# Nine dummy products, first loads on two queues, and a last token tile summed in two halves of its columns, in a two-layer hybrid encoder

## The chip, the cores and the metric

The kernel runs on 1 core of one Trainium2 chip. The metric is the time on the device in microseconds (us) from one launch to its end. Each kernel was run several times; the number that stands for it is the median. One further execution was recorded by the hardware profiler, and every row of a view below comes from that one.

## The reference

A trunk of two layers works on one stream x of 256 tokens by 2048 features, all in 32-bit floats.

```python
def even_layer(x, ...):                       # layer 0
    hn = rmsnorm(x, norm_g)
    q, k, v, u, z_a, z_b = jnp.split(hn @ w_in, cuts, axis=-1)   # 1024 columns each
    o_a = chunked_relpos_attention(q, k, v, rel_bias) * jax.nn.silu(z_a)
    y = jax.nn.gelu(s5_ssm(u, lam_re, lam_im, log_dt, b_re, b_im, c_re, c_im, d_skip))
    o_b = y * jax.nn.sigmoid(y @ w_glu + b_glu) * jax.nn.silu(z_b)
    return x + jnp.concatenate([o_a, o_b], axis=-1) @ w_out

def odd_layer(x, ...):                        # layer 1
    hn = rmsnorm(x, norm_g)
    q, k, v, z, f_logit = jnp.split(hn @ w_in, cuts, axis=-1)    # 2048 columns each, 16 for f
    log_f = jax.nn.log_sigmoid(f_logit + b_forget)
    o = forgetting_attention(q, k, v, log_f) * jax.nn.silu(z)
    return x + o @ w_out

out = rmsnorm(odd_layer(even_layer(x)), final_norm_g)
```

`s5_ssm` is a state space model: 64 groups of 16 channels of u, each with 64 complex states that a recurrence over the 256 tokens carries on. The large matrices (w_in of both layers, w_out of both, w_glu) are what the kernel streams from memory; the attention, the recurrence and the norms are small beside them.

## The kernel before

**Tiling.** The tokens lie in two tiles of 128 (t = 0 and 1). A weight matrix is read in column blocks of 512 (`NT`); along the 2048 rows it comes in chunks of two blocks of 128 rows (`CK`), so one chunk is a tile of 128 x 1024 numbers, 512 KB. `next_w` loads the next chunk on SyncE's (SP's) queue into `wr` (4 buffers), and splits it into a rounded part `wh` (ScalarE, ACT, L164) and the rest `wl` (VectorE, DVE, L165), 3 buffers each. Where an activation has been split in the same way (`xTh`, `xTl`), the product in full precision is the sum of three products on TensorE (PE): high by high (L175), high by low (L176), low by high (L177). `project` makes these for 16 blocks of rows and both token tiles and adds them up in two accumulators of 128 x 512; every name `acc_...` is one of these. A chunk feeds 12 products.

**Front.** The first chunk comes in two halves of 256 KB (`split`), each with its own splits, so that the first products can start sooner. `gE` is the norm's weight; `x_block` scales the transposed x (`xTr`) by it and splits it (L215, L216). The norm's factor for each token is applied later, to the sums. All these loads stand on SP. The S5 part reads its parameters (`lr`, `li`, `dt`, `dcol`) through GpSimd's (POOL's) queue in `s5_setup`.

**Order.** PE runs its instructions in the order in which the program is written. On the other engines a scheduler lays them out when the kernel is built, by modelled times, and gives the splits a high priority. Work beside the stream of weights is cut into tasks; `tick` advances one step after each chunk, and `at_chunk` places a task on that clock. Such a task's products stand on PE between two chunks.

**The order of the work up to 100 us.** First come the two column blocks of u (`acc_u`). Their sums are scaled into `ut` tiles (one to a token tile and column block) and stored to a buffer `u_d` in memory (L743 and L747). Four loads on SP read it back in another layout as `un` (L439), ACT reorders it (L446, `spread`), and PE transposes it (`pu`, L456). Beside this run the tables of the S5 part (`tables`): DVE computes `mx` (L378 to L380), which SP stores (`m_d`, L381); PE multiplies it with `bb` into `pk` (L395); DVE and ACT make `ks` of that, which SP stores as `k_d` (L402); loads of `bc` (L340) for a later table stand behind these stores on SP, and ACT scales them (L356). Meanwhile PE goes on with the projections for za (`acc_za`) and then q.

**The tail.** The last projection is w_out of layer 1, its last column block with `by_token=True`: its eight chunks are held ready, and the 48 products of tile 0 are made before the 48 of tile 1. Then `add_tile` adds the sum to x (L997) and squares it on ACT (L999), and the final norm's factor follows in five small steps (`ms`, `r` by a power on POOL, `c`, `rc`, L1022 to L1027). The last 512 columns (`xg`) and the three other column blocks are multiplied by `rc` and stored, four stores of 256 KB on SP to a token tile (L1034).

Of the kernel before, what the change touches and what calls it, by code (L numbers as in the profile page):

```python
# [9 lines left out]
F32 = mybir.dt.float32  # L10
F32R = mybir.dt.float32r
AF = mybir.ActivationFunctionType
# [5 lines left out]
P = 128  # L18
L = 256
# [18 lines left out]
PI_F = 3.1415925  # L38
SPLIT_AHEAD = 3000
SCAN_SLOW, S5_OUT = 79, 95  # L40


@with_exitstack
def trunk(ctx: ExitStack, tc: tile.TileContext, a, out: bass.AP):
# [8 lines left out]

    ctx.enter_context(tc.manual_schedule(engines={mybir.EngineType.PE}))

    warm = const.tile([P, 1], F32, name="warm")
    nc.vector.memset(warm, 0.0)
    nc.scalar.activation(warm, warm, AF.Exp)
    gE = const.tile([P, 16], F32, name="gE")
    nc.sync.dma_start(gE, a["gE"])  # L60
    xin = a["x"].rearrange("(t p) d -> p t d", p=P)

    ident = const.tile([P, P], F32, name="ident")
# [84 lines left out]
    def next_w(split=None, dst=None):  # L148
# [8 lines left out]
        step = NT if split else CK * NT  # L157
        for o in range(0, CK * NT, step):
            c = slice(o, o + step)
            nc.sync.dma_start(raw[:, c], a["w"][i][:, c])  # L160
            if split:
                split(o // NT)
            with tc.high_priority(offset=SPLIT_AHEAD):
                last_split[:] = [nc.scalar.activation(wh[:, c], raw[:, c], AF.Copy)]  # L164
                nc.vector.tensor_tensor(wl[:, c], raw[:, c], wh[:, c].bitcast(F32), op=ALU.subtract)  # L165
        return wh, wl

    def project(ah, al, nkb, name, evac, ready=None, by_token=False):
# [8 lines left out]
            nc.tensor.matmul(acc[t], sl, wh[:, c], start=False, stop=kb == nkb - 1)  # L177

        if by_token:
            for t in range(2):  # L180
                for kb in range(nkb):
                    block(kb, *ready[kb // CK], t)
            return acc
        for kc in range(nkb // CK):
            wh, wl = ready[kc] if ready else next_w()
            kbs = range(kc * CK, (kc + 1) * CK)
# [70 lines left out]
    cr = sm("cr")  # L257
    csn = s5.tile([P, 2, G], F32, name="csn")
    kst = [s5.tile([P, 2, 2 * P], F32, name=f"ks{i}") for i in range(2)]
    e2 = s5b.tile([P, 2, G], F32, name="e2")  # L260
    e1t = s5b.tile([P, G], F32, name="e1t")

    def s5_setup():
        for h in range(2):
            nc.gpsimd.dma_start(lr[h * 64:(h + 1) * 64, :], a["s5lr"])
            nc.gpsimd.dma_start(li[h * 64:(h + 1) * 64, :], a["s5li"])
        nc.gpsimd.dma_start(dt, a["s5dt"].to_broadcast([P, G]))
        dcol = s5.tile([P, NGQ], F32, name="dcol")
        nc.gpsimd.dma_start(dcol, a["s5d"])
        for t_ in kst:  # L270
            nc.gpsimd.memset(t_[:, :, 0:P], 0.0)

        V.memset(sgn[0:64, :], -1.0)
        V.memset(sgn[64:128, :], 1.0)
        V.memset(nsgn[0:64, :], 1.0)
# [740 lines left out]
    held = [next_w(dst=(lh[:, i, :], ll[:, i, :]) if i < 4 else None if i < 7 else lx) for i in range(8)]  # L1016
    acc = project(oTh, oTl, 16, "oo3", None, held, by_token=True)
    for t in range(2):
        xs = add_tile(3, acc[t], t)
        xg = l1.tile([P, NT], F32, name=f"xg_{t}", tag="xg")  # L1020
        nc.vector.tensor_tensor(xg, xs, gF[:, 3 * NT:], op=ALU.mult)
        ms, r, c, rc = (const.tile([P, 1], F32, name=f"{w}_2{t}") for w in ("ms", "rs", "rc", "rr"))  # L1022
        nc.vector.scalar_tensor_tensor(ms, ssp2[:, t, 3:4], 1.0 / D, s012[:, t:t + 1], op0=ALU.mult, op1=ALU.add)
        nc.gpsimd.tensor_tensor(r, ms, mhalf[:, 0:1], op=ALU.pow)
        nc.vector.tensor_scalar(c, ms, r, r, op0=ALU.mult, op1=ALU.mult)
        nc.vector.tensor_scalar(c, c, -0.5, 1.5, op0=ALU.mult, op1=ALU.add)
        nc.vector.tensor_tensor(rc, r, c, op=ALU.mult)  # L1027
        for n in (2, 3, 0, 1):
            xs = x[:, t, n * NT:(n + 1) * NT] if n < 3 else xg
            if n == 2:  # L1030
                nc.scalar.activation(xs, xs, AF.Copy, scale=rc)
            else:
                nc.vector.tensor_scalar(xs, xs, rc, None, op0=ALU.mult)
            nc.sync.dma_start(ov[:, t, n * NT:(n + 1) * NT], xs)  # L1034

# [75 lines left out]
```

## Time and profile before

| | before |
|---|---|
| runs, us | 968.22, 966.23, 968.06 |
| median, us | 968.06 |
| the profiled execution's own time, us | 967.27 |
| its span (first to last instruction), us | 965.6 |
| mean granted clock of PE, as a share of full speed | 0.99 |
| moved by the DMA engines | 190.43 MB, 197 GB/s on average |

The profile's second part cuts the span into 40 slices of 24.1 us and gives the busy share of an engine in tenths (9 is 90% or more):

```
PE   6997999999998999999999999999999999999995
ACT  6636556864464666455645644464446444644451
PEclk9999999999999899999999999999999999999998
DMA  9877566645999468655556555555554556455552
```

PE's lower digits stand in the first slice, in the fourth (72 to 97 us), in the thirteenth (290 to 314 us) and in the last. In the views, a row of the timeline has the start and the length of an instruction in us, its engine, line, operation, and what it writes and reads; a bracket gives the idle time before it and what ended that. A length of a product on PE runs from its issue to its end, and products overlap: what one costs is the distance to the next one's start, not its length.

### The profile page before, as it was taken

To read this page: it belongs to the slowest core of one execution; us is meant where nothing else is said; L and a number is where in the kernel's file an instruction comes from. 1 tells how busy PE (TensorE), PEld (TensorE's weight loads), DVE (VectorE), ACT (ScalarE), POOL (GpSimd) and SP (SyncE) were. 2 spreads that over 40 slices of the span, in tenths; PEclk is the share of its full clock that TensorE was granted. 3 is DMA by queue.
4 is the path that set the end of the run, shared out by engine and by line. 5 is a ranking of instruction groups with operands and counts; after the bars stand their busy time and mean duration, and the time that the engine had idled before them with its cause. 6 is when DMAs were issued, how large, how long until landed. Compare 5 with 4: busy or idle time off the path is not lost.

```text
span 965.6 us, 13241 instructions
## 1 busy us (share of the span) xinstructions
PE 933.5 (97%) x4814; PEld 758.8 (79%) x4814; DVE 579.4 (60%) x1023; ACT 517.0 (54%) x817; POOL 104.4 (11%) x177
## 2 busy tenths in 40 slices
PE   6997999999998999999999999999999999999995
PEld 5885777777776678788888888888888888888884
DVE  7886678755798346665755545454545454545573
ACT  6636556864464666455645644464446444644451
POOL 2000000000652000200001400040004000200210
PEclk9999999999999899999999999999999999999998
DMA  9877566645999468655556555555554556455552
GB/s 326 289 222 230 178 203 203 193 156 185 227 232 305 161 224 247 219 174 182 179 195 226 174 186 174 190 171 186 173 193 148 184 173 194 152 182 171 195 197 88
DMA packets 68546, 190.43 MB, mean 197 GB/s; under 512 B 7936, under 2 KB 22512, under 8 KB 68096
## 3 DMA queue, kind: packets, MB, share of 16 engines
q1 hardware_dynamic: 65056, 181.07, 58.4%
q0 software_dynamic: 3424, 8.51, 3.5%
q8 instruction: 38, 0.62, 0.3%
q14 instruction: 28, 0.23, 0.1%
HBM read 180.09 MB, written 9.45 MB: 196 GB/s over the span
## 4 chain that ended last, share of the span: by engine, by line
PE 85%; DVE 4%; DMA 3%; ACT 3%; issue 3%; SPq 1%; POOL 0%; POOLq 0%; DVEq 0%; ACTq 0%
PE acc_cq L175 3%; PE acc_cv L177 3%; PE acc_ck L175 3%; PE acc_cq L177 3%; PE acc_cv L176 3%; PE acc_cz L177 3%; PE acc_cv L175 3%; PE acc_cq L176 3%; PE acc_cz L175 3%; PE acc_ck L177 3%; PE acc_ck L176 3%; PE acc_cz L176 3%; PE acc_oo L177 3%; PE acc_oo L175 3%; PE acc_oo L176 3%
## 5 line engine op out<-in xcount | busy, mean ns | idle before, releaser
L165 DVE TENSOR_TENSOR wl<-wr,wh 128x1024 fp32r<-128x1024 f32 (+1 forms) x292 | 361.4, 1238 | 288.1 <-ACT wh L164 287.4
L164 ACT ACTIVATE wh<-wr 128x1024 fp32r<-128x1024 f32 (+1 forms) x292 | 310.9, 1066 | 342.4 <-PE acc_cz L177 46.7
L175 PE MATMUL acc_cv<-wh,x1Th 128*128 128x512 f32 x128 | 51.3, 400 | 0.0
L175 PE MATMUL acc_cq<-wh,x1Th 128*128 128x512 f32 x128 | 50.6, 395 | 0.0
L175 PE MATMUL acc_cz<-wh,x1Th 128*128 128x512 f32 x128 | 50.2, 392 | 0.0
L177 PE MATMUL acc_cv<-wh,x1Tl 128*128 128x512 f32 x128 | 50.0, 390 | 0.0
L176 PE MATMUL acc_cv<-wl,x1Th 128*128 128x512 f32 x128 | 49.9, 390 | 0.0
L175 PE MATMUL acc_ck<-wh,x1Th 128*128 128x512 f32 x128 | 49.9, 390 | 0.0
L177 PE MATMUL acc_cq<-wh,x1Tl 128*128 128x512 f32 x128 | 49.9, 390 | 0.0
L176 PE MATMUL acc_cq<-wl,x1Th 128*128 128x512 f32 x128 | 49.8, 389 | 0.0
L177 PE MATMUL acc_cz<-wh,x1Tl 128*128 128x512 f32 x128 | 49.8, 389 | 0.0
L177 PE MATMUL acc_ck<-wh,x1Tl 128*128 128x512 f32 x128 | 49.8, 389 | 0.0
L176 PE MATMUL acc_ck<-wl,x1Th 128*128 128x512 f32 x128 | 49.8, 389 | 0.0
L176 PE MATMUL acc_cz<-wl,x1Th 128*128 128x512 f32 x128 | 49.8, 389 | 0.0
L916 POOL TENSOR_SCALAR cbt<-ckb,cum 128x128 f32<-128x128 f32 x16 | 13.8, 861 | 308.8 <-DVE mx_c L529 261.9
L175 PE MATMUL acc_oo<-wh,oTh 128*128 128x512 f32 x108 | 42.2, 391 | 0.0
L177 PE MATMUL acc_oo<-wh,oTl 128*128 128x512 f32 x108 | 42.0, 389 | 0.0
L176 PE MATMUL acc_oo<-wl,oTh 128*128 128x512 f32 x108 | 42.0, 389 | 0.0
L636 POOL DMA_DIRECT2D T<-k_d x64 | 33.6, 530 | 58.3 <-DMA k_d<-ks 37.0
L175 PE MATMUL acc_u<-wh,xTh 128*128 128x512 f32 x64 | 26.0, 406 | 6.0 <-ACT wh L164 6.0
L175 PE MATMUL acc_q<-wh,xTh 128*128 128x512 f32 x64 | 26.8, 418 | 2.3 <-ACT za L500 2.2
L175 PEld LDWEIGHTS acc_ck<-wh,x1Th 128*128 128x128 f32 x128 | 24.0, 188 | 5.4 <-ACT wh L164 0.4
(407 smaller groups left out, 2080.0 us busy)
## 6 DMA issues: line engine op xcount, KB each, us to landing
wr<-in_w_dram SPq DMA_DIRECT2D x295, 512.0 KB, 3.4
m_d<-mx SPq DMA_DIRECT2D x8, 512.0 KB, 5.7
T<-k_d POOLq DMA_DIRECT2D x64, 64.0 KB, 6.8
mo<-m_d POOLq DMA_DIRECT2D x8, 512.0 KB, 7.2
bt<-in_rbx_dram SPq DMA_DIRECT2D x8, 256.0 KB, 7.6
bc<-in_s5bc_dram SPq DMA_DIRECT2D x8, 256.0 KB, 4.0
xt<-in_x_dram SPq DMA_DIRECT2D x2, 1024.0 KB, 7.2
xa<-in_x_dram SPq DMA_DIRECT2D x4, 512.0 KB, 6.6
```

The lines of the kernel that those rows point to most:

```text
L164: last_split[:] = [nc.scalar.activation(wh[:, c], raw[:, c], AF.Copy)]
L165: nc.vector.tensor_tensor(wl[:, c], raw[:, c], wh[:, c].bitcast(F32), op=ALU.subtract)
L175: nc.tensor.matmul(acc[t], sh, wh[:, c], start=kb == 0, stop=False)
L176: nc.tensor.matmul(acc[t], sh, wl[:, c], start=False, stop=False)
L177: nc.tensor.matmul(acc[t], sl, wh[:, c], start=False, stop=kb == nkb - 1)
L636: nc.gpsimd.dma_start(tt_[j * GC:(j + 1) * GC], k_d[e, :, :, GC * (j + 1):GC * (j + 1) + P])
L916: W.tensor_scalar(bt[:, 0, :], self.ckb[:, hh, 0:P], cum[:, 0, h:h + 1], None, op0=ALU.add)
```

## The change

Line numbers of the kernel after are some 17 higher than before. The change has four parts.

1. **Dummy products.** Nine products of zeros by zeros, 128 x 128 x 128 in 32-bit floats, into a tile `idle` that nobody reads, stand first on PE. The zeros are the padding of `kst`, which had been cleared later on POOL and is now cleared at once, one tile on DVE and one on POOL.
2. **Two queues.** `gE` and the first half of the first chunk are loaded on ACT's queue; ACT's first activation (Exp, which loads its function table) is put behind these issues. The S5 parameters are still loaded on POOL's queue, but only after POOL has copied one column of `xr`'s block 7, that is, once the third `xTr` load has landed.
3. **Last tile in halves.** Tile 1 of the last projection is summed in 96 products of 256 columns, all of the left half before the right half, into two accumulators; tile 0 stays as it was.
4. **Tail.** The steps of the last column block run on whole rows for t = 0, and for t = 1 on each half, with the sum of squares added up from two parts. `xg` is multiplied by `r` and `c` in one step without waiting for `rc`, and its store is the first of four instead of the third; the store of block 2 moves to ACT's queue.

```diff
@@ -38,6 +38,7 @@
 PI_F = 3.1415925
 SPLIT_AHEAD = 3000
 SCAN_SLOW, S5_OUT = 79, 95
+WARM = 9
 
 
 @with_exitstack
@@ -53,11 +54,10 @@
 
     ctx.enter_context(tc.manual_schedule(engines={mybir.EngineType.PE}))
 
+    gE = const.tile([P, 16], F32, name="gE")
+    nc.scalar.dma_start(gE, a["gE"])
     warm = const.tile([P, 1], F32, name="warm")
     nc.vector.memset(warm, 0.0)
-    nc.scalar.activation(warm, warm, AF.Exp)
-    gE = const.tile([P, 16], F32, name="gE")
-    nc.sync.dma_start(gE, a["gE"])
     xin = a["x"].rearrange("(t p) d -> p t d", p=P)
 
     ident = const.tile([P, P], F32, name="ident")
@@ -157,7 +157,9 @@
         step = NT if split else CK * NT
         for o in range(0, CK * NT, step):
             c = slice(o, o + step)
-            nc.sync.dma_start(raw[:, c], a["w"][i][:, c])
+            (nc.scalar if split and o == 0 else nc.sync).dma_start(raw[:, c], a["w"][i][:, c])
+            if split and o == 0:
+                nc.scalar.activation(warm[:, 0:1], warm[:, 0:1], AF.Exp)
             if split:
                 split(o // NT)
             with tc.high_priority(offset=SPLIT_AHEAD):
@@ -177,10 +179,19 @@
             nc.tensor.matmul(acc[t], sl, wh[:, c], start=False, stop=kb == nkb - 1)
 
         if by_token:
-            for t in range(2):
+            for kb in range(nkb):
+                block(kb, *ready[kb // CK], 0)
+
+            halves = [acc[1][:, 0:NT // 2], ps_acc.tile([P, NT], F32, name=f"acc_{name}_2", tag="acc")[:, 0:NT // 2]]
+            for h in range(2):
                 for kb in range(nkb):
-                    block(kb, *ready[kb // CK], t)
-            return acc
+                    wh, wl = ready[kb // CK]
+                    c = slice(kb % CK * NT + h * NT // 2, kb % CK * NT + (h + 1) * NT // 2)
+                    sh, sl = ah[:, kb, P:L], al[:, kb, P:L]
+                    nc.tensor.matmul(halves[h], sh, wh[:, c], start=kb == 0, stop=False)
+                    nc.tensor.matmul(halves[h], sh, wl[:, c], start=False, stop=False)
+                    nc.tensor.matmul(halves[h], sl, wh[:, c], start=False, stop=kb == nkb - 1)
+            return [acc[0]], halves
         for kc in range(nkb // CK):
             wh, wl = ready[kc] if ready else next_w()
             kbs = range(kc * CK, (kc + 1) * CK)
@@ -257,19 +268,25 @@
     cr = sm("cr")
     csn = s5.tile([P, 2, G], F32, name="csn")
     kst = [s5.tile([P, 2, 2 * P], F32, name=f"ks{i}") for i in range(2)]
+
+    zero = kst[0][:, 0, 0:P]
+    V.memset(kst[0][:, :, 0:P], 0.0)
+    nc.gpsimd.memset(kst[1][:, :, 0:P], 0.0)
+    idle = ps_s.tile([P, P], F32, name="idle", tag="s")
+    for _ in range(WARM):
+        nc.tensor.matmul(idle, zero, zero, start=True, stop=True)
     e2 = s5b.tile([P, 2, G], F32, name="e2")
     e1t = s5b.tile([P, G], F32, name="e1t")
 
     def s5_setup():
-        for h in range(2):
-            nc.gpsimd.dma_start(lr[h * 64:(h + 1) * 64, :], a["s5lr"])
-            nc.gpsimd.dma_start(li[h * 64:(h + 1) * 64, :], a["s5li"])
-        nc.gpsimd.dma_start(dt, a["s5dt"].to_broadcast([P, G]))
         dcol = s5.tile([P, NGQ], F32, name="dcol")
-        nc.gpsimd.dma_start(dcol, a["s5d"])
-        for t_ in kst:
-            nc.gpsimd.memset(t_[:, :, 0:P], 0.0)
-
+
+        with tc.issue_after(nc.gpsimd.tensor_copy(lr[:, 0:1], xr[:, 7, 0:1]).ins):
+            for h in range(2):
+                nc.gpsimd.dma_start(lr[h * 64:(h + 1) * 64, :], a["s5lr"])
+                nc.gpsimd.dma_start(li[h * 64:(h + 1) * 64, :], a["s5li"])
+            nc.gpsimd.dma_start(dt, a["s5dt"].to_broadcast([P, G]))
+            nc.gpsimd.dma_start(dcol, a["s5d"])
         V.memset(sgn[0:64, :], -1.0)
         V.memset(sgn[64:128, :], 1.0)
         V.memset(nsgn[0:64, :], 1.0)
@@ -1016,22 +1033,32 @@
     held = [next_w(dst=(lh[:, i, :], ll[:, i, :]) if i < 4 else None if i < 7 else lx) for i in range(8)]
     acc = project(oTh, oTl, 16, "oo3", None, held, by_token=True)
     for t in range(2):
-        xs = add_tile(3, acc[t], t)
+        nh = 1 + t
         xg = l1.tile([P, NT], F32, name=f"xg_{t}", tag="xg")
-        nc.vector.tensor_tensor(xg, xs, gF[:, 3 * NT:], op=ALU.mult)
         ms, r, c, rc = (const.tile([P, 1], F32, name=f"{w}_2{t}") for w in ("ms", "rs", "rc", "rr"))
-        nc.vector.scalar_tensor_tensor(ms, ssp2[:, t, 3:4], 1.0 / D, s012[:, t:t + 1], op0=ALU.mult, op1=ALU.add)
+        for h in range(nh):
+            cs = slice(h * NT // nh, (h + 1) * NT // nh)
+            xs = x[:, t, 3 * NT + cs.start:3 * NT + cs.stop]
+            nc.vector.tensor_tensor(xs, acc[t][h], xs, op=ALU.add)
+            sq = l1.tile([P, NT], F32, name=f"sq2_3_{t}_{h}", tag="cqkT")
+            part = const.tile([P, 1], F32, name=f"part_{t}_{h}")
+            nc.scalar.activation(sq[:, cs], xs, AF.Square, accum_out=part)
+            nc.vector.tensor_tensor(xg[:, cs], xs, gF[:, 3 * NT + cs.start:3 * NT + cs.stop], op=ALU.mult)
+            nc.vector.scalar_tensor_tensor(ms, part, 1.0 / D, s012[:, t:t + 1] if h == 0 else ms,
+                                           op0=ALU.mult, op1=ALU.add)
         nc.gpsimd.tensor_tensor(r, ms, mhalf[:, 0:1], op=ALU.pow)
         nc.vector.tensor_scalar(c, ms, r, r, op0=ALU.mult, op1=ALU.mult)
         nc.vector.tensor_scalar(c, c, -0.5, 1.5, op0=ALU.mult, op1=ALU.add)
+        nc.vector.tensor_scalar(xg, xg, r, c, op0=ALU.mult, op1=ALU.mult)
+        nc.sync.dma_start(ov[:, t, 3 * NT:], xg)
         nc.vector.tensor_tensor(rc, r, c, op=ALU.mult)
-        for n in (2, 3, 0, 1):
-            xs = x[:, t, n * NT:(n + 1) * NT] if n < 3 else xg
+        for n in (2, 0, 1):
+            xs = x[:, t, n * NT:(n + 1) * NT]
             if n == 2:
                 nc.scalar.activation(xs, xs, AF.Copy, scale=rc)
             else:
                 nc.vector.tensor_scalar(xs, xs, rc, None, op0=ALU.mult)
-            nc.sync.dma_start(ov[:, t, n * NT:(n + 1) * NT], xs)
+            (nc.scalar if n == 2 else nc.sync).dma_start(ov[:, t, n * NT:(n + 1) * NT], xs)
 
 
 
```

The scheduler laid out the rest of the program anew, too. Three places follow, before and then after.

DVE from the fourth chunk on (the `ve_dt` rows are steps of an exponential of `dt`; `ddiag` is a table from `dcol`; the `wl` rows are splits of successive chunks, `wl_165` of the fifth). Before:

```order
L216 SCALAR_TENSOR_TENSOR xTl<-xTr,gE,xTh 128x256 x8
L87 TENSOR_SCALAR ve_dt<-dt 128x64
L88 TENSOR_SCALAR ve_dt<-ve_dt 128x64
L89 TENSOR_SCALAR ve_dt<-ve_dt 128x64
L281 TENSOR_TENSOR ddiag<-dmask,dcol 128x256
L165 TENSOR_TENSOR wl_165<-wr_163,wh_164 128x1024
```

After:

```order
L227 SCALAR_TENSOR_TENSOR xTl<-xTr,gE,xTh 128x256 x8
L167 TENSOR_TENSOR wl_165<-wr_163,wh_164 128x1024
L87 TENSOR_SCALAR ve_dt<-dt 128x64
L88 TENSOR_SCALAR ve_dt<-ve_dt 128x64
L89 TENSOR_SCALAR ve_dt<-ve_dt 128x64
L167 TENSOR_TENSOR wl_171<-wr_169,wh_170 128x1024
```

The split `wl_165` moved ahead of the `ve_dt` steps, and `ddiag` went three splits later.

SP where u leaves and comes back. Chunks have other numbers in the two programs: `wr_741`, `wr_809`, `wr_831`, `wr_854`, `wr_900` and `wr_932` of before are `wr_752`, `wr_820`, `wr_842`, `wr_865`, `wr_911` and `wr_943` of after; `ut_216` and `ut_217` (after: `ut_228` and `ut_229`) are the two token tiles of u. Before:

```order
L747 DMA u_d<-ut_217 128x512
L160 DMA wr_741<-in_w_dram 128x1024
L747 DMA u_d<-ut_217 128x512
L743 DMA u_d<-ut_216 128x512 x2
L160 DMA wr_809<-in_w_dram 128x1024
L439 DMA un<-u_d 32x8x256 x2
L160 DMA wr_831<-in_w_dram 128x1024
L439 DMA un<-u_d 32x8x256 x2
L160 DMA wr_854<-in_w_dram 128x1024
L160 DMA wr_900<-in_w_dram 128x1024
L381 DMA m_d<-mx_558 1024x1x128
```

After:

```order
L760 DMA u_d<-ut_228 128x512
L764 DMA u_d<-ut_229 128x512
L160 DMA wr_752<-in_w_dram 128x1024
L760 DMA u_d<-ut_228 128x512
L764 DMA u_d<-ut_229 128x512
L456 DMA un<-u_d 32x8x256 x4
L160 DMA wr_820<-in_w_dram 128x1024
L160 DMA wr_842<-in_w_dram 128x1024
L160 DMA wr_865<-in_w_dram 128x1024
L160 DMA wr_911<-in_w_dram 128x1024
L160 DMA wr_943<-in_w_dram 128x1024
L398 DMA m_d<-mx_569 1024x1x128
```

The four `un` loads now stand together, ahead of two loads of chunks that had stood before them and between them; and the store of `m_d`, which came one row after `wr_900`, comes one row after `wr_943`, the next chunk.

DVE around the first `mx` (the rows of `w_1` and `tw` belong to the next table). Before:

```order
L379 TENSOR_TENSOR tm_559<-pi,bc_383 128x1024
L165 TENSOR_TENSOR wl_743<-wr_741,wh_742 128x1024
L380 TENSOR_TENSOR mx_558<-mx_558,tm_559 128x8x128
L165 TENSOR_TENSOR wl_811<-wr_809,wh_810 128x1024
L371 TENSOR_TENSOR tw_797<-psg,bb_789 128x8x112
L165 TENSOR_TENSOR wl_833<-wr_831,wh_832 128x1024
L370 TENSOR_TENSOR w_1_796<-pr,bb_789 128x8x112
L165 TENSOR_TENSOR wl_856<-wr_854,wh_855 128x1024
L378 TENSOR_TENSOR mx_802<-pr,bc_385 128x8x128
L372 TENSOR_TENSOR w_1_796<-w_1_796,tw_797 128x8x112
L400 TENSOR_TENSOR ks_211<-pk_772,ddiag 128x2x16
```

After:

```order
L396 TENSOR_TENSOR tm_570<-pi,bc_394 128x1024
L167 TENSOR_TENSOR wl_822<-wr_820,wh_821 128x1024
L397 TENSOR_TENSOR mx_569<-mx_569,tm_570 128x8x128
L167 TENSOR_TENSOR wl_844<-wr_842,wh_843 128x1024
L388 TENSOR_TENSOR tw_808<-psg,bb_800 128x8x112
L387 TENSOR_TENSOR w_1_807<-pr,bb_800 128x8x112
L167 TENSOR_TENSOR wl_867<-wr_865,wh_866 128x1024
L395 TENSOR_TENSOR mx_813<-pr,bc_396 128x8x128
L417 TENSOR_TENSOR ks_211<-pk_783,ddiag 128x2x16
```

The last step of `mx` stood behind the split of `wr_741`; now it stands behind the split of `wr_820`, one chunk later. `ks` stood behind the split of the fourth chunk in this piece; now it stands behind that of the third, directly after one step of the next `mx`.

## The prediction

> **What bounds the kernel.** I read the page first, then PE's waits, then the windows of the first 100 us.
>
> ```profile
> PE 933.5 (97%) x4814; PEld 758.8 (79%) x4814; DVE 579.4 (60%) x1023; ACT 517.0 (54%) x817; POOL 104.4 (11%) x177
> ```
>
> PE is busy 97% of the span, so time can only come from its idle stretches, from slow-clock stretches, from the front and from the tail. PE's waits, in us, how many, the longest:
>
> ```profile
> PE pp_a L547 <- ACT lg_a L539: 5.8, 1, 5.8
> PE pu L456 <- ACT un L446: 5.1, 1, 5.1
> PE acc_za L176 <- DVE wl L165: 0.8, 1, 0.8
> PE acc_za L175 <- ACT wh L164: 0.7, 1, 0.7
> ```
>
> The last three lie between 75 and 93 us, where the diff's words touch nothing. pp_a's (around 316 us) stands behind tasks that PE's own progress releases, so I let it move with PE. In the windows (length, busy time of PE, PEld, DVE, ACT, POOL, granted clock, DMA share, GB/s):
>
> ```profile
> 10.00:20.00 10.00, 9.28 (x39) 7.07 (x38) 8.78 (x19) 9.08 (x16) 0.40 (x2) 1.00 1.03 393
> 90.00:100.00 10.00, 7.12 (x29) 5.87 (x30) 4.54 (x6) 6.81 (x11) 0.21 (x1) 0.83 0.57 194
> ```
>
> From 10 to 20 us the DMA engines are full (share 1.03). From 90 to 100 the clock granted is 0.83: after pu's wait PE restarts slowly, which costs (1 - 0.83) x 10 = 1.7 us at most.
>
> **The front.** Rows of the timeline (start, length):
>
> ```profile
> 0.80 0.39 SPq L60 DMA_DIRECT2D gE<-in_gE_dram  x1
> 1.24 0.42 SPq L220 DMA_DIRECT2D xTr<-in_xT_dram  x1
> 6.04 0.79 PE L175 MATMUL acc_u<-wh,xTh 128*128 128x512 f32 x1 [6.04 <-ACT wh L164]
> 9.06 0.63 PE L175 MATMUL acc_u<-wh,xTh 128*128 128x512 f32 x1
> 9.49 0.63 PE L176 MATMUL acc_u<-wl,xTh 128*128 128x512 f32 x1
> 12.31 0.51 PE L176 MATMUL acc_u<-wl,xTh 128*128 128x512 f32 x1 [0.72 <-DVE wl L165]
> 12.65 0.40 PE L177 MATMUL acc_u<-wh,xTl 128*128 128x512 f32 x1
> 18.89 1.06 ACT L164 ACTIVATE wh<-wr 128x1024 fp32r<-128x1024 f32 x1 [0.46 <-DMA wr<-in_w_dram]
> 20.31 1.22 DVE L165 TENSOR_TENSOR wl<-wr,wh 128x1024 fp32r<-128x1024 f32 x1
> 21.59 0.50 PE L176 MATMUL acc_u<-wl,xTh 128*128 128x512 f32 x1 [0.60 <-DVE wl L165]
> ```
>
> gE leaves SP, so the first xTr load is issued 1.24 - 0.80 = 0.44 us earlier, and with it the data, wh and the first real matmul (5.6 instead of 6.04). Products start 0.43 us apart at 9 us, against lengths of 0.40 that overlap at 12.65: the clock comes up some 4.3 us after PE starts. Nine dummies from about 1.3 us, each two passes (0.22 us by the rows on poc below, 0.45 on the slow clock), fill 4.0 us; so the real products run fast from the start, and the dummies cost nothing, since PE had nothing else. But that speed alone buys nothing: the second chunk's wl ended PE's wait at 12.31 with data from full DMA engines, and PE will only wait longer there. What is kept is set by the last wait of this stretch, at 21.59: wl started at 20.31 though wh was done at 18.89 + 1.06 = 19.95, because three ve_dt steps and ddiag stood before it on DVE. In the new order it stands ahead of them: 0.36 us, plus the 0.44: **PE leads by 0.8 us** at 21.6 (0.4 if the data gain nothing; 1.3 if taking the small s5 loads out of the way counts too). The moved loads issue on POOL after xr's eighth block; dt is needed at about 20.7, and the loads of before took 4 to 6.5 us, so I charge nothing; a late dt would stall DVE, with wl behind it.
>
> On two queues: full engines (1.03 above) leave only issue time to win. [...]
>
> **The middle.** The scheduler laid out the new program differently from 30 to 80 us (the pieces of order above). The rows of before (landing rows: KB, us from issue; wr was issued at 65.45, behind two un; the m_d rows are its first, at 68.55, and second):
>
> ```profile
> 56.96 1.05 SPq L743 DMA_DIRECT2D u_d<-ut  x2
> 64.08 1.31 SPq L439 DMA_DIRECT2D un<-u_d  x2
> ```
>
> ```profile
> wr<-in_w_dram SPq DMA_DIRECT2D x1, 512.0 KB, 5.6
> m_d<-mx SPq DMA_DIRECT2D x1, 512.0 KB, 9.2
> m_d<-mx SPq DMA_DIRECT2D x1, 512.0 KB, 5.8
> bc<-in_s5bc_dram SPq DMA_DIRECT2D x1, 256.0 KB, 4.6
> ```
>
> ```profile
> 65.67 1.22 DVE L380 TENSOR_TENSOR mx<-mx,tm 128x1024 f32<-128x1024 f32 x1
> 71.83 0.64 PE L395 MATMUL pk<-mx,bb 128*32 128x128 f32 x16
> 73.92 1.14 ACT L446 COPY un<-un 128x512 f32<-128x512 f32 x2 [5.52 <-DMA un<-u_d]
> 81.47 0.18 DVE L400 TENSOR_TENSOR ks<-pk,ddiag 128x32 f32<-128x32 f32 x1
> 89.32 0.40 ACT L356 ACTIVATE bc<-bc,nsgn 128x128 f32<-128x128 f32 x1 [6.27 <-DMA bc<-in_s5bc_dram]
> 92.19 0.64 ACT L446 COPY un<-un 128x512 f32<-128x512 f32 x1
> 92.88 2.12 PE L456 MATMUL pu<-ident,un 128*128 128x128 f32 x8 [5.15 <-ACT un L446]
> ```
>
> Before: ACT stood 5.52 us at 73.92 for un, with wh behind it; that made PE's 0.7 and 0.8. ks came at 81.47, then k_d, bc, ACT's bc at 89.32, un, pu at 92.88: 11.4 us after ks, which I keep.
>
> After: the ut_0 stores go out before ut_1's last, so the last store is issued near 55.5 instead of 57.5. The load that stood behind them goes behind un: 512 KB, 1.3 us at 393 GB/s; I take 1.0. **un is issued from 64.08 - 2.0 - 1.0 = 61.0** (60 to 64). Four un take 4 x 0.65 = 2.6, so the next wr goes at 63.6; behind four un instead of two I take 6.4 instead of 5.6: 70.0. wh 1.06, wl 1.22, then mx 1.22, which now stands behind that wl on DVE: 73.5. So **a new wait**: PE reaches pk at 71.83 - 0.8 = 71.0 and stands 2.5 us, where 1.5 goes; queued behind pk are the next za products. m_d is issued at 73.6; with one load ahead of it I take 5.2, between bc's 4.6 and m_d's 5.8: 78.8. The next mx (1.22) and ks directly after it give ks at 80.0 instead of 81.47 + 0.18: **1.6 us earlier, and pu with it** (3.5 earlier with un at 60 and 4.6; 2.4 later with 9.2). PE's lead of 0.8 is swallowed in that wait, since ks does not hang on it. PE reaches pu after 73.5 + 14.5 = 88.0 and waits 3.2 instead of 5.15, so its clock may stay up: 0.4 of the 1.7 is my share. From there the order on every engine is the old one, and I let it all shift.
>
> **The tail.** t = 1 is summed in 96 products of 256 columns instead of 48 of 512. A 256-column product starts 0.12 us after the other, and full 128x128 weight loads come 0.11 apart:
>
> ```profile
> 487.49 0.28 PE L853 MATMUL pf<-x1Tl,wfx 128*32 128x256 f32 x1
> 487.61 0.28 PE L852 MATMUL pf<-x1Th,wfx 128*32 128x256 f32 x1
> 578.37 0.30 PEld L939 LDWEIGHTS poc<-cv,pT_c 128*128 128x128 f32 x2
> 578.60 0.30 PEld L940 LDWEIGHTS poc<-cv,pT_c 128*128 128x128 f32 x2
> ```
>
> 96 x 0.114 = 10.9 us is what 48 x 0.227 were: 0. The last products' chain is then half as wide. Its rows, and two tiles' lengths at 512 and 1024 columns (shortest, median, longest ns):
>
> ```profile
> L164 ACT ACTIVATE wh<-wr x11: 614/1059/1065, 5.4 to 29.9; 128x1024 fp32r<-128x1024 f32 x9, 128x512 fp32r<-128x512 f32 x2
> L165 DVE TENSOR_TENSOR wl<-wr,wh x10: 691/1218/1226, 6.0 to 28.3; 128x1024 fp32r<-128x1024 f32 x8, 128x512 fp32r<-128x512 f32 x2
> ```
>
> ```profile
> 955.88 0.69 DVE L997 TENSOR_TENSOR xr<-acc_oo,xr 128x512 f32<-128x512 f32 x1 [6.57 <-PE acc_oo L177]
> 956.66 0.63 ACT L999 ACTIVATE sq<-xr 128x512 f32<-128x512 f32 x1 [7.84 <-DVE xr L997]
> 958.75 0.16 DVE L1027 TENSOR_TENSOR rr<-rs,rc 128x1 f32<-128x1 f32 x1
> 959.46 0.33 SPq L1034 DMA_DIRECT2D out_dram<-xg  x1
> ```
>
> 256 columns less: DVE (1218 - 691)/2 = 0.26, ACT (1059 - 614)/2 = 0.22; rr leaves the path of xg: 0.2. The first store comes 0.7 us earlier, and the other three follow 0.43 apart or closer. **0.7** (0.4 if the last store lags; 1.2 if ACT's queue spares a turn).
>
> **Sum**, against the profiled 967.27 (0.8 under the median of the runs, 968.06): 967.27 - 1.6 - 0.4 - 0.7 = **964.6**.
>
> **Rivals.**
> 1. The middle gives nothing. un waits as long as before, or m_d takes 9.2: pu near 93, the new wait eats what the old ones free, and only the tail is left: 966.6. For it: pk's new wait is as sure as the order, and m_d's two rows differ by 3.4 us. Against: two loads fewer are in flight ahead of m_d.
> 2. Slower: weight loads set the pace of the narrow products. If a load of 0.30 - 0.11 = 0.19 us cannot hide behind 0.11 of streaming, 96 x 0.19 = 18.2 instead of 10.9: 7.3 us more, 964.6 + 7.3 = 971.9. It decides against the change from 0.15 us a product on. Against: poc's loads start 0.11 apart. [...]
> 3. The dummies don't lift the clock (zeros, or too few): chunk one runs slow, but the 21.59 wait hides it, so at most the 0.8 lead is lost, ahead of a wait that swallows it anyway: 964.6 to 965.4. It would show in the trace, hardly in the time.
> 4. The middle goes well: ks 3.5 us earlier and the clock stays up: 967.27 - 3.5 - 1.5 - 0.7 = 961.6.
>
> **Chances.** Forecast 0.50, rival 1 0.25, rival 2 0.05, rival 3 0.05, rival 4 0.15. From rival 4 less 1 to rival 1 plus 0.8: 960.6 to 967.4, leaving out rival 2 and the worst of rival 1. A measurement of this kernel tells about 0.2% (1.9 us) from none: forecast, 3 and 4 pass it against the median when they hold (0.68 of 0.70), rival 1 mostly not: faster 0.70, same 0.23, slower 0.07.
>
> **What would show it.** First real matmul near 5.6 us, lengths of 0.40 before 9 us (the dummies); 21.59 near 20.8 (front); un issued near 61, ACT not standing for un, PE waiting for mx at pk, ks near 80, pu's wait near 3 us (middle); starts 0.114 us apart at the end and the first store 2.9 us after the last product instead of 3.6 (tail). Wrong if un is issued at 64 or later, if m_d lands after 82, or if waits past 100 us grow.

## The result, and the profile after

The kernel after ran at a median of 961.06 us (957.87 to 962.55, 5 runs) against 967.76 us (965.52 to 968.22, 5 runs) for the kernel before, a ratio of 0.9934 with a 95% interval of 0.9911 to 0.9957. Measured once more beside other kernels (e5 below) the ratio was 0.9948 (0.9929 to 0.9967). So the change is worth 5 to 7 us; the prediction had 3.5 against the median of before. The time lies at the lower edge of the predicted range (960.6 to 967.4), below even what rival 4 gave for a middle that goes well (961.6). The profiled execution took 960.76 us with a span of 959.0, 6.6 us less than the 965.6 of before.

The page's first part, of the kernel after: PE's busy time is 933.5 us, as before. But 4.2 us of it are now the dummies, which fill what had been idle. So of the 6.6 us, 4.2 are a shorter busy time of the other products and 2.4 are shorter waits and a shorter end.

```profile
PE 933.5 (97%) x4880; PEld 762.9 (80%) x4880; DVE 579.8 (60%) x1027; ACT 516.2 (54%) x819; POOL 107.8 (11%) x177
```

PE's waits, after (us in total, how many, the longest). Lines stand some 17 higher than before:

```profile
PE pp_a L564 <- ACT lg_a L556: 5.8, 1, 5.8
PE pk L412 <- DVE mx L397: 3.3, 1, 3.3
PE acc_u L178 <- DVE wl L167: 1.5, 3, 0.8
PE acc_q L177 <- ACT za L517: 1.4, 1, 1.4
PE pu L473 <- ACT un L463: 1.3, 2, 1.0
PE acc_u L177 <- ACT wh L166: 1.1, 1, 1.1
```

pu's wait of 5.1 us has shrunk to 1.3, the two on za's splits are gone, and a new one of 3.3 us stands at pk: the wait that the prediction named. To see where the time goes, one reads the start of the same PE instruction in both timelines and takes the difference, the **lead** of the kernel after:

| place on PE | before, us | after, us | lead | forecast |
|---|---|---|---|---|
| first za product, after all of u | 54.14 | 53.03 | 1.1 | 0.8 |
| first pk product | 71.83 | 74.05 | -2.2 | -1.7 |
| first pv product (the step after pu) | 100.94 | 97.15 | 3.8 | 2.0 |
| pm of a later table | 214.02 | 207.99 | 6.0 | 2.0 |
| last product of all | 955.45 | 949.59 | 5.9 | 2.0 |
| end of the span | 965.6 | 959.0 | 6.6 | 2.7 |

**Front, after.** Rows of the timeline (start, length; in brackets the idle time before it and what ended that):

```profile
1.28 4.21 PE L277 MATMUL idle<-ks 128*128 128x128 f32 x18 [1.28 <-DVE ks L273]
6.60 0.50 PE L177 MATMUL acc_u<-wh,xTh 128*128 128x512 f32 x1 [1.11 <-ACT wh L166]
7.66 0.40 PE L179 MATMUL acc_u<-wh,xTl 128*128 128x512 f32 x1
7.90 0.39 PE L177 MATMUL acc_u<-wh,xTh 128*128 128x512 f32 x1
20.28 0.50 PE L178 MATMUL acc_u<-wl,xTh 128*128 128x512 f32 x1 [0.77 <-DVE wl L167]
```

```profile
4.62 0.91 ACT L226 ACTIVATE xTh<-xTr,gE 128x256 fp32r<-128x256 f32 x2 [1.40 <-DMA gE<-in_gE_dram]
5.92 1.15 ACT L166 ACTIVATE wh<-wr 128x512 fp32r<-128x512 f32 x2 [0.39 <-DMA wr<-in_w_dram]
```

Behind the dummies (nine in the program, 18 instructions of PE in the trace, 4.21 us) real products start 0.22 to 0.24 us apart from 7.66 us on (waits aside), where those of before started 0.43 us apart until 10.3 us. But the first starts at 6.60 us instead of 6.04, since ACT had to wait for gE (1.40 us) and for the first half chunk (0.39 us), the two loads that went to its own queue. What remains is the wait at 20.28 instead of 21.59. Its chunk's splits, after:

```profile
17.91 1.06 ACT L166 ACTIVATE wh<-wr 128x1024 fp32r<-128x1024 f32 x1 [1.02 <-DMA wr<-in_w_dram]
19.00 1.23 DVE L167 TENSOR_TENSOR wl<-wr,wh 128x1024 fp32r<-128x1024 f32 x1 [1.05 <-ACT wh L166]
```

wh starts 1.0 us earlier (17.91 instead of 18.89), and wl follows it 0.03 us after its end instead of 0.36.

**Middle, after.** SP, ACT and DVE, then PE:

```profile
61.18 2.61 SPq L456 DMA_DIRECT2D un<-u_d  x4
63.84 9.38 SPq L160 DMA_DIRECT2D wr<-in_w_dram  x5
74.02 0.59 SPq L398 DMA_DIRECT2D m_d<-mx  x1
80.39 2.87 SPq L419 DMA_DIRECT2D k_d<-ks  x4
```

```profile
70.55 1.06 ACT L166 ACTIVATE wh<-wr 128x1024 fp32r<-128x1024 f32 x1 [7.73 <-DMA wr<-in_w_dram]
```

```profile
72.78 1.22 DVE L397 TENSOR_TENSOR mx<-mx,tm 128x1024 f32<-128x1024 f32 x1
80.18 0.18 DVE L417 TENSOR_TENSOR ks<-pk,ddiag 128x32 f32<-128x32 f32 x1
```

```profile
74.05 1.08 PE L412 MATMUL pk<-mx,bb 128*32 128x128 f32 x16 [3.29 <-DVE mx L397]
90.10 0.66 PE L473 MATMUL pu<-ident,un 128*128 128x128 f32 x4 [1.00 <-ACT un L463]
97.15 0.64 PE L431 MATMUL pv<-min,uT 128*32 128x128 f32 x16
```

Read downwards this is one chain: un at 61.18 puts the next chunk's load at 63.84, its split at 70.55, mx at 72.78, m_d at 74.02, ks at 80.18. The m_d store landed in 4.9 us (9.2 before, when it went out at 68.55 behind other loads). The clock dropped behind pk's wait this time and not behind pu's, by the windows (length, busy PE, PEld, DVE, ACT, POOL, clock, DMA share, GB/s):

```profile
70.00:80.00 10.00, 6.71 (x40) 5.12 (x39) 7.60 (x7) 6.37 (x11) 0.00 (x0) 0.83 0.91 302
90.00:100.00 10.00, 9.55 (x75) 7.44 (x76) 4.91 (x5) 6.79 (x15) 0.21 (x1) 1.00 0.60 199
```

**Tail, after.** The start of the narrow products, the last one, the first store:

```profile
938.24 0.28 PE L191 MATMUL acc_oo<-lh,oTh 128*128 128x256 f32 x1
949.59 0.28 PE L193 MATMUL acc_oo<-lx,oTl 128*128 128x256 f32 x1
```

```profile
952.82 0.33 SPq L1053 DMA_DIRECT2D out_dram<-xg  x1
```

From the last product's end (949.59 + 0.28) the store is issued 2.95 us later; before it was 3.61.

### The profile page after: what moved, and what is told of

It is laid out like the page before. It is cut to its first block, busy times and chain, and to the rows that moved or that the text cites. A ratio compares the mean times of both kernels' runs of the same rounds, so it can differ in the third digit from the quotient of the medians.

```text
span 959.0 us, 13377 instructions
## 1 busy us (share of the span) xinstructions
PE 933.5 (97%) x4880; PEld 762.9 (80%) x4880; DVE 579.8 (60%) x1027; ACT 516.2 (54%) x819; POOL 107.8 (11%) x177
## 4 chain that ended last, share of the span: by engine, by line
PE 86%; DMA 4%; DVE 4%; issue 3%; ACT 2%; SPq 0%; POOL 0%; POOLq 0%; ACTq 0%; DVEq 0%
PE acc_cq L177 3%; PE acc_cv L179 3%; PE acc_ck L177 3%; PE acc_cq L179 3%; PE acc_cv L178 3%; PE acc_cv L177 3%; PE acc_cq L178 3%; PE acc_cz L179 3%; PE acc_ck L179 3%; PE acc_cz L177 3%; PE acc_ck L178 3%; PE acc_cz L178 3%; PE acc_oo L177 3%; PE acc_oo L178 3%; PE acc_oo L179 3%
## 5 line engine op out<-in xcount | busy, mean ns | idle before, releaser
L177 PE MATMUL acc_oo<-wh,oTh 128*128 128x512 f32 x102 | 39.9, 391 | 0.0
L179 PE MATMUL acc_oo<-wh,oTl 128*128 128x512 f32 x102 | 39.7, 389 | 0.0
L178 PE MATMUL acc_oo<-wl,oTh 128*128 128x512 f32 x102 | 39.7, 389 | 0.0
L179 PEld LDWEIGHTS acc_cq<-wh,x1Tl 128*128 128x128 f32 x128 | 24.0, 188 | 5.1
L179 PEld LDWEIGHTS acc_cv<-wh,x1Tl 128*128 128x128 f32 x128 | 24.0, 188 | 5.0
```

The lines of the kernel that those rows point to most:

```text
L177: nc.tensor.matmul(acc[t], sh, wh[:, c], start=kb == 0, stop=False)
L178: nc.tensor.matmul(acc[t], sh, wl[:, c], start=False, stop=False)
```

## The experiments

Each kernel was timed beside the kernel before. Eight of them take one part of the change alone (tail e1, S5 loads e2, dummies e9, queues e10) or leave one out (e4, e12, e3, e11).

**e1, the tail alone.** The kernel before with the diff's last two places:

```diff
+            halves = [acc[1][:, 0:NT // 2], ps_acc.tile([P, NT], F32, ...)[:, 0:NT // 2]]
...
+        nh = 1 + t
```

> The kernel before with the two column halves and the new tail alone; the order on every engine up to 900 us is that of before. Theory (the gain comes from the middle, which the scheduler laid out anew): the narrow products cost 0.5 us, the tail saves 0.65, so the time is within 0.3 us of before plus the noise of the clock waits: ratio 0.999 to 1.001, pu's wait about 5 us and acc_q's 2.2 as before. Rival (the tail is the larger part of the 6.6 us): 3 us or more faster, ratio 0.997 or less.

Measured: 0.9988 (0.9976 to 1.0001). Not told from before, as the theory had it; the rival is out. The wait of acc_q missed: 3.3 us, not 2.2. From the first product of tile 1 to the end of the span its profile has 963.0 - 942.16 = 20.84 us; before has 965.6 - 944.75 = 20.85. Up to that product every engine has the same instructions in the same order in both profiles, and e1's reached it 2.6 us earlier: so much one profile can differ from another without any change.

**e2, the late S5 loads alone.** The kernel before with

```diff
+        with tc.issue_after(nc.gpsimd.tensor_copy(lr[:, 0:1], xr[:, 7, 0:1]).ins):
```

> The kernel before with the late S5 loads alone: no dummies, one queue, old tail. The scheduler then lays out the middle as in the kernel after (four un loads together ahead of two chunks, mx one split later). Theory: most of the gain is there, since pu's wait falls from 5 us to near 1 and the wait at 207 us no longer drops the clock: 4.5 to 6.5 us faster than before, ratio 0.9935 to 0.9955; a wait of 2 to 4 us appears at pk. Rival (the early front, dummies and two queues, is what pulls the middle forward): no more than 2 us, ratio above 0.998.

Measured: 0.9995 (0.9983 to 1.0007). The theory falls: the new order alone brings nothing that can be told. Its profile has a wait at pk (4.5 us) and a small one at pu (0.7), as in the kernel after, but un was issued at 63.93 us, not at 61, and pv started at 100.00.

**e3, no dummy products.** The kernel after with

```diff
-    for _ in range(WARM):
-        nc.tensor.matmul(idle, zero, zero, start=True, stop=True)
```

> The kernel after without the nine dummy products (the zeros are still cleared). Leaves no part of the result out. Theory: the first chunk runs at the slow clock, starts 0.4 us apart to about 11 us, but the waits for the second and fourth chunk's splits hide that, and the wait at pk swallows what is left: PE's lead at pk and after the same within 0.3 us, time equal to after within 0.5 us. Rival (the products buy the 1.1 us of lead and it lasts): 1 us slower than after.

Measured: 0.9967 (0.9952 to 0.9982), a median of 963.12 us. The slow start is there (0.43 us apart from 7.73 to 10.72 us), and the lead of the front was not lost: the first za product started at 52.74 us, a lead of 1.4. The first rows of its timeline:

```profile
6.41 0.79 PE L177 MATMUL acc_u<-wh,xTh 128*128 128x512 f32 x1 [6.41 <-ACT wh L166]
9.01 0.63 PE L179 MATMUL acc_u<-wh,xTl 128*128 128x512 f32 x1
9.44 0.63 PE L177 MATMUL acc_u<-wh,xTh 128*128 128x512 f32 x1
```

But un was issued only at 62.60, so at pk the lead was -3.5 us (after: -2.2), and pv started at 98.78. So both miss: the products don't buy the lead, as the rival had it, and what stands behind it was not equal to after, as the theory had it.

**e4, the old tail.** The kernel after with the two places of e1 undone.

> The kernel after with the last tile in one piece and the old tail. Theory: the narrow products give back 0.5 and the old tail costs 0.65 to 0.8: 0.1 to 0.3 us slower than after in a profile with the same waits, not to be told from after by time (958 to 963). Rival (the tail is the larger part): 3 us slower, 964 or more.

Measured: 0.9965 (0.9950 to 0.9980), 961.89 us, as the theory had it. Its profiled span is 959.5, 0.5 us more than after's, but none of that comes from the tail: from the first product of tile 1 to the end it has 959.5 - 938.73 = 20.77 us, after 959.0 - 938.24 = 20.76.

**e5, the kernel after again,** unchanged.

> The kernel after once more, beside the other three. In the profiles of after, e2, e3 and e4 the first pv product starts 36.0, 36.1, 36.2 and 35.7 us after the first un load is issued, though those issues lie between 61.0 and 63.9 us. Theory (in the new layout everything from 60 to 100 us hangs on that issue): pv again 35.7 to 36.2 us after it; the time 0.991 to 0.997 of before. Rival (chance): a distance outside 35 to 37 us.

Measured: 0.9948, as told above; un at 61.51, pv at 97.23, 35.7 us later. As expected.

**e6, un behind the next chunk.** The kernel after with the un loads later in the program and tied behind the last chunk's load:

```diff
+        yield 7
+        with tc.issue_after(last_w[0].ins):
             for g4 in range(4):
                 nc.sync.dma_start(un[32 * g4:32 * g4 + 32], ...)
```

> The kernel after with the four un loads one place later on SP, behind the load of the next chunk; all else in order. Theory (the load of that chunk, its splits and then mx wait behind un, and this makes the wait of 3.3 us at pk): the chunk is loaded near 58 us instead of 63.8, mx is ready before PE comes, the wait at pk is gone, the next one at pu stays under 2 us, the first pv starts at 93.5 to 95 instead of 97.2: 2 to 4 us faster than after. Rival (the chain from ks through k_d and bc to pu ends last whatever stands before it): pu waits 3 to 5 us instead, pv near 97, time as after.

Measured: 0.9935 (0.9915 to 0.9955), a median of 958.93 us (957.63 to 959.65), the lowest of all, but not told from e5's 960.12. The wait at pk is gone, as the theory had it; pv (at 96.85) and the time are as the rival had them, but pu waited 1.3 us, not 3 to 5. Other places took over what pk no longer waits for. PE of e6 (the second row is the pu that waits for bc):

```profile
80.65 0.50 PE L177 MATMUL acc_q<-wh,xTh 128*128 128x512 f32 x1 [1.21 <-ACT za L518]
88.16 0.66 PE L474 MATMUL pu<-ident,un 128*128 128x128 f32 x4 [1.33 <-ACT un L465]
```

and m_d, issued at 69.88 behind four chunk loads, landed in 7.4 us instead of 4.9. This pu came 1.9 us earlier than after's (90.10), but from it to pv it took 8.7 us instead of 7.05, with a granted clock of 0.67 from 90 to 95 us. This profile's front was also 1.1 us later than after's (first za product at 54.15); from there to pv it took 42.7 us against 44.1.

**e7, the old order on SP.** The kernel after with the stores of u and the un loads tied to the places of before:

```diff
+            with tc.issue_after(st.ins):
+                for t_ in range(2):
+                    nc.sync.dma_start(u_d[t_ * P:(t_ + 1) * P, 0:NT], us[0][:, t_, :])
...
+            if g4 == 2:
+                yield 1
+            with tc.issue_after(last_w[0].ins):
```

> The kernel after with the stores of u, the un loads and the two chunks between them put back on SP in the order of before; front and tail stay as after. Theory A (the place of the stores and of un is what brought the gain of the middle): un is issued at 62.5 to 63.5, pu waits 4 to 5 us again, the first pv starts at 99 to 101, 2 to 4 us slower than after. Theory B (PE's lead of 1.1 us from the front is what moved everything): un near 62.5, but pv at 97 to 98 and time within 1 us of after.

Measured: 0.9956 (0.9942 to 0.9970), 960.68 us, beside e5's 960.12; pv at 97.77. Theory A falls, B holds. un was issued at 61.72 in the old order too. The waits only moved: none at pk, but one of 3.1 us where PE waits until ACT has read the sums of za (a row of PE), while m_d, issued at 68.64, took 9.3 us to land:

```profile
81.33 0.50 PE L177 MATMUL acc_q<-wh,xTh 128*128 128x512 f32 x1 [3.12 <-ACT za L520]
```

**e8, no halves.** The kernel after with tile 1 in 48 products and `nh = 1`.

> The kernel after with tile 1 of the last projection summed in 48 products of 512 columns; the order of the new tail stays. Theory: PE ends 0.5 us earlier and DVE's and ACT's steps on 512 columns take 0.5 us more, so from the first to the last of the 48 products and on to the end of the span nothing changes by more than 0.2 us; time as after. Rival (the halves are worth what the prediction gave them): 0.5 us or more slower.

Measured: 0.9957 (0.9942 to 0.9973), 960.56 us. From the first product of tile 1 to the end 958.8 - 938.06 = 20.74 us; after has 959.0 - 938.24 = 20.76. The halves are worth nothing.

**e9, the dummies alone, and e10, the two queues alone.** The kernel before with

```diff
+    for _ in range(WARM):
+        nc.tensor.matmul(idle, zero, zero, start=True, stop=True)
```

> The kernel before with the nine dummy products alone (and the earlier clearing of their zeros); the scheduler again puts the four un loads together. Theory (what counts up to 100 us is when un is issued, and the products do not move that): PE's lead at the first za product 0.3 us or less, un issued at 62 to 64 us, the first pv product 35.5 to 36.5 us after it, time 0.997 to 1.001 of before. Rival (the fast clock in the first chunk is what the front gains): lead 0.8 us or more at the first za product, 0.993 to 0.996.

and the kernel before with

```diff
-    nc.sync.dma_start(gE, a["gE"])
+    nc.scalar.dma_start(gE, a["gE"])
...
-            nc.sync.dma_start(raw[:, c], a["w"][i][:, c])
+            (nc.scalar if split and o == 0 else nc.sync).dma_start(raw[:, c], a["w"][i][:, c])
```

> The kernel before with gE and the first half chunk on ACT's queue alone. Theory: the first product starts within 0.5 us of before's 6.0, the lead at the first za product is 0 to 0.5 us, un issued at 62 to 64 us, pv 35.5 to 36.5 us later, time 0.996 to 1.001 of before. Rival (two queues carry the front's 1.1 us): lead 0.8 us or more, 0.993 to 0.996.

Measured: e9 0.9985 (0.9974 to 0.9997), leads at za and pv 0.2 and -0.5; e10 0.9981 (0.9970 to 0.9992), first product at 6.63, leads -0.2 and 4.1. Both are inside the theory's ranges of time, and both rivals are out. The distance from un to pv missed in both (39.4 and 37.8 us, not 35.5 to 36.5), and e10's un went out at 59.06 already; in both the stores of u have an order of their own, with one chunk's load between them and un.

**e11, one queue, and e12, early S5 loads:** the kernel after with the diff of e10, and with that of e2, undone.

> The kernel after with gE and the first half chunk back on SP. If two queues are worth their issue time: lead at the first za product 0.4 to 0.7 us instead of 1.1, un 0.4 to 0.7 us later, time within 1 us of after, 0.994 to 0.998 of before. If they carry the front: lead 0.2 or less, 0.997 or more.

> The kernel after with the S5 loads back at the start. If the late loads are what gives the front its lead (the small loads out of the way of the first chunks, and dt's steps behind the split of the fifth): lead at the first za product 0.4 us or less, un 0.7 to 1.2 us later than in after, time 0.996 to 0.999 of before. If not: lead 0.9 us or more, 0.9935 to 0.9955, as after.

Measured: e11 0.9967 (0.9953 to 0.9980), lead at za 0.0, un at 63.37; e12 0.9950 (0.9936 to 0.9965), lead at za 0.8, un at 59.56 but pv at 99.74. By the lead, two queues carry the front, though alone (e10) they give none; by time e11 falls into the first of its cases and just short of the 0.997 of the second, and its un came 2.2 us later than after's, not 0.4 to 0.7. e12's lead lies between its two cases, its un came earlier and not later, and its time is that of after.

Together, from the timelines (the lead against before; the wait runs from the end of the last store's issue to un's issue; pu is the first one behind bc). The seven rows from after to e2 have after's order on SP; e7 and e1 have that of before up to the un loads, and the last four have orders of their own:

| kernel | lead at first za | stores to un | un issued | un to pv | pu to pv | lead at pv | ratio of times |
|---|---|---|---|---|---|---|---|
| before | 0 | 6.1 | 64.08 | 36.9 | 8.1 | 0 | 1 |
| after | 1.1 | 4.6 | 61.18 | 36.0 | 7.1 | 3.8 | 0.9934 |
| e5 after again | 1.0 | 5.0 | 61.51 | 35.7 | 7.1 | 3.7 | 0.9948 |
| e4 old tail | 1.1 | 4.3 | 61.03 | 35.7 | 7.1 | 4.2 | 0.9965 |
| e8 no halves | 1.6 | 4.3 | 60.97 | 35.8 | 7.1 | 4.1 | 0.9957 |
| e3 no products | 1.4 | 6.8 | 62.60 | 36.2 | 7.1 | 2.2 | 0.9967 |
| e11 one queue | 0.0 | 4.1 | 63.37 | 35.5 | 7.0 | 2.1 | 0.9967 |
| e2 S5 loads alone | -0.2 | 6.7 | 63.93 | 36.1 | 7.1 | 0.9 | 0.9995 |
| e7 old order | 1.2 | 4.9 | 61.72 | 36.1 | 8.7 | 3.2 | 0.9956 |
| e1 tail alone | 0.3 | 4.6 | 62.35 | 38.3 | 9.4 | 0.3 | 0.9988 |
| e6 un behind chunk | 0.0 | 4.8 | 62.49 | 34.4 | 8.7 | 4.1 | 0.9935 |
| e9 dummies alone | 0.2 | 3.4 | 61.98 | 39.4 | 8.7 | -0.5 | 0.9985 |
| e10 two queues alone | -0.2 | 2.1 | 59.06 | 37.8 | 7.1 | 4.1 | 0.9981 |
| e12 early S5 loads | 0.8 | 3.1 | 59.56 | 40.2 | 8.6 | 1.2 | 0.9950 |

The lead at pv does not settle the time: e10 has 4.1 us there and a ratio of 0.9981, e12 has 1.2 and 0.9950.

## Why the prediction held, and where its steps did not

**The sign and the place were right, in part by luck.** The middle was to give most, by way of un: issued at 61.0 (measured 61.18), mx ready at 73.5 (74.0), a new wait of 2.5 us at pk (3.3), m_d in 5.2 us (4.9), ks at 80.0 (80.18). All hold within 0.8 us. But the two terms behind un's 61.0 did not come out as they stood. The order of the stores was to bring the last one 2.0 us forward; it was issued 1.3 us earlier (56.20 instead of 57.5), and the front's lead is 1.1 of that. e2, with the new order and no lead, has 0.7. The load behind un was to give 1.0; the wait from the stores to un became 1.5 us shorter, but in e2 it is longer than before, and in e1, the program of before up to the tail, it is as short as in after.

**The step that failed: "PE's lead of 0.8 is swallowed in that wait, since ks does not hang on it".** It does hang on it, by way of un. In the seven profiles with after's order on SP (after, e2, e3, e4, e5, e8, e11) pv starts 35.5 to 36.2 us after un's issue, though that issue lies between 60.97 and 63.93; and un waits for the stores of u, which wait for PE's sums. So the front's lead can go through un, mx and ks to pv. How much of it arrives is not shown: e3, with a lead of 1.4, and e11, with none, both have about 2.1 us at pv, since the wait from the stores to un was 6.8 us in one and 4.1 in the other. The order that I had taken for the cause gives little by itself: e2, which has it without the lead, is at 0.9995, and e7, which has the lead without it, at 0.9956 beside e5's 0.9948. The first store of mx went out at 68.64 in e7 and took 9.3 us to land; in after it went out at 74.02 and took 4.9: 5.4 us between the issues, 1.0 between the landings (77.9 and 78.9). So the wait at pk cost little that e7, without it, did not lose at the store. The rest of the difference is the wait from the stores to un. Before and e1 show that it scatters with no change at all: 6.1 and 4.6 us in the same program. Which part of a difference of such size belongs to a kernel stays open.

**From ks to pv.** Of the lead of 3.8 us at pv, 1.3 stood at ks (81.47 - 80.18), 1.5 came between ks and pu, and 1.0 between pu and pv; the forecast had 1.6, 0 and 0.4. Its 1.6 compared a start (80.0) with an end (81.47 + 0.18); from start to start it is 1.5. I kept 11.4 us from ks to pu; it took 90.10 - 80.18 = 9.9. bc alone took 1.4 us less to land: issued at 83.32, used by ACT at 86.54; before, 84.69 and 89.32. Of the clock's 1.7 us I gave 0.4 to the change; from pu to pv it took 7.05 us instead of 8.06. The drop of the clock had moved to the wait at pk (0.83 from 70 to 80 us), where it cost nothing at pv: ks came directly behind an mx step that had waited for m_d, and PE still stood 1.0 us at pu. All seven profiles with after's order have 7.0 to 7.1 us from pu to pv. Before, e1, e6, e7, e9 and e12 have 8.1 to 9.4, and their windows from 90 to 95 us show a clock of 0.54 to 0.88. The length of the wait at pu alone does not decide it: e10 had 2.7 us and no drop (7.1 us from pu to pv), e6 had 1.3 and a drop (0.67 from 90 to 95 us).

**"From there the order on every engine is the old one, and I let it all shift" missed 2.2 us.** Between pv and the pm at 208 us the lead grew from 3.8 to 6.0. Before, and then after:

```profile
207.25 0.50 PE L175 MATMUL acc_q<-wh,xTh 128*128 128x512 f32 x1 [2.20 <-ACT za L500]
208.84 1.91 PE L506 MATMUL pz<-ident,za 128*128 128x128 f32 x8
```

```profile
202.87 0.50 PE L177 MATMUL acc_q<-wh,xTh 128*128 128x512 f32 x1 [1.42 <-ACT za L517]
204.36 1.04 PE L523 MATMUL pz<-ident,za 128*128 128x128 f32 x8
```

The wait is 0.8 us shorter, and there is no drop of the clock behind it (1.00 from 200 to 210 us, where before has 0.86 from 205 to 210 and 0.80 from 210 to 215; pz in 1.04 us, not 1.91), to which I put the other 1.4 us. The shorter wait recurs: it is 1.4 to 1.6 us in e3, e4, e5, e8 and e11, and 2.2 and 3.3 in before and e1. The second part is no gain that can be counted on: e1, the same program as before up to there and with a wait of 3.3 us, shows no drop at this place (1.00 from 205 to 215 us). Runs of before scatter from 962.65 to 968.78 us beside e5, and e1's profile is 2.6 us ahead of before's by the same program, so the ratio of 0.9948 is a better measure than the 6.6 us of the two profiles.

**The front: right in sum, wrong in its way.** 0.8 us was forecast and 1.1 came. But I had the first product at 5.6 us through the earlier issue, and it came later than before, 6.60. With gE and the half chunk on ACT's queue it started at 6.3 to 6.7 us in nine profiles, with all on SP at 5.9 to 6.3 in five. The lead comes from the chunks behind it. At the wait that was to decide it, 1.3 us were gained: 1.0 by the earlier wh, where I had 0.44 from the earlier issue, and 0.3 by the place of wl on DVE, where I had 0.36. SP gave up two issues, of which I had counted only gE's: its first load of a whole chunk was issued at 2.18 instead of 3.13. But that is not enough by itself, for e10 issues it at 2.17 and has no lead. At the first za product the lead is 1.0 to 1.6 in six of the seven profiles with two queues and late S5 loads together (0.0 in e6), 0.8 with two queues and early loads beside the dummies (e12), and at most 0.3 in the other five. What the dummies do was forecast rightly as to the lead (e3 has 1.4 without them). As to the time it isn't settled: alone they give 0.9985 (0.9974 to 0.9997), and without them the ratio is 0.9967 beside 0.9948, two ratios whose intervals overlap; no profile here shows a mechanism by which they would save time.

**The tail: the sum was 0.7, and it is 0.1 or less.** The chain at the end became shorter as forecast (2.95 us instead of 3.61). But the narrow products start (949.59 - 938.24) / 95 = 0.1195 us apart, where I had taken 0.114 from weight loads although the two rows quoted above them said 0.12; 96 of them cost 11.47 us, the 48 wide ones (955.45 - 944.75) / 47 x 48 = 10.93. So 0.54 of the 0.7 were given back. From the first product of tile 1 to the end, before has 20.85 us and e1, with the new tail, 20.84; e4, with the old one, has 20.77 and after 20.76. Rival 2, weight loads that set the pace, is out: by its price the products would have started 0.19 us apart. In the profile of after their weight loads do take 0.19 us each (means of 188 to 192 ns on PEld, L191 to L193), and the products start 0.12 us apart all the same.

**The parts.** Alone they give 0.12 (tail), 0.05 (S5 loads), 0.15 (dummies) and 0.19% (queues), in sum 0.51; the whole gives 0.52 in e5. That agrees with parts that simply add, but does not show it: each part is known to about 0.12% either way, the first two are not told from nothing, and for the tail the profiles show 0.1 us or less where 0.12% would be 1.2.

## What to carry to other kernels

A wait that appears where the lead of an earlier stage seems to end need not swallow that lead: follow what the late operand itself hangs on, back across stores and loads, to the engine whose lead is in question. When a store lands says more than when it goes out: the first store of mx went out at 68.6 to 69.9 us in before, e7 and e6 and took 7.4 to 9.3 us, went out at 74.0 in after and took 4.9, and so landed only 1.0 to 1.6 us earlier in those three. Between e7 and after, PE's wait moved (3.1 us at acc_q, 3.3 at pk) more than it changed in length. And a shorter end chain that is bought with more instructions is to be priced at the distance of starts measured for just that width: 0.0055 us on each of 96 products took back most of 0.7. Before two profiles are compared, one program should be profiled twice: here two profiles of the same instructions lay 2.6 us apart, about as much as the whole forecast (2.7).

## What the runs showed of the hardware that was not expected

- Two loads moved from SP's to ACT's queue were issued at the same time or earlier, but took longer to land: gE took 1.6 us from issue to landing on SP (before) and 3.8 on ACT (after), the first half chunk 3.6 and 4.7. In after SP issued a load at the same time as each of the two, so how much is the queue and how much the company is not shown.
- Behind 4.2 us of products of zeros (after) real products started 0.22 to 0.24 us apart from 7.66 us on (waits aside); in before, whose first product is a real one at 6.04 us, they did so from 10.72 on. The slow start of before (0.43 us apart to 10.3 us), which the prediction put down to the clock, shows only in the distance of starts: the windows from 6 to 11 us have a granted clock of 1.00 in it.
- Waits of like length were or were not followed by a drop of the clock: 2.2 us (before, 207 us) and 2.3 us (e10, same place) were, 2.1 us (e2, clock 1.00 from 205 to 215 us) and 3.3 us (e1) there were not; pk's 3.3 us (after) was (0.90 from 70 to 75 us, 0.76 from 75 to 80). The rows of before, e10 and e1 for the windows behind that wait:

```profile
205.00:210.00 5.00, 2.80 (x13) 2.35 (x13) 1.96 (x4) 4.97 (x11) 0.20 (x1) 0.86 0.29 105
```

```profile
205.00:210.00 5.00, 5.00 (x21) 4.21 (x20) 1.96 (x3) 3.15 (x7) 0.00 (x0) 0.68 0.39 126
```

```profile
210.00:215.00 5.00, 5.00 (x45) 4.08 (x44) 2.49 (x4) 4.56 (x9) 0.00 (x0) 1.00 0.45 130
```
